# Hybrid attention step: the second weight block's split one token tile later and half of it on VectorE, the third tile's low parts ahead of the fourth tile's scaling, three filler products fewer

## The chip, the cores and the metric

The kernel runs on one core of a Trainium2 chip. The metric is the device time of one execution in microseconds (us). Three runs of the kernel before gave 967.75, 967.85 and 968.23 us; the median is 967.85 us.

## The reference, cut to what matters

One layer of a streaming encoder: RMS norm, one input projection, two kinds of attention, gates, an output projection and the residual. The change touches only the first part, in which 1024 prompt tokens and 64 sample tokens are normed and multiplied by the first two blocks of `w_in` columns:

```python
def rms_norm(x, w):
    xf = x.astype(jnp.float32)
    ms = jnp.mean(xf * xf, axis=-1, keepdims=True)
    return (xf * lax.rsqrt(ms + EPS)).astype(x.dtype) * w
...
    h = rms_norm(x, norm_w) @ w_in
    sb_q, sb_k, sb_v, sb_z, cb_q, cb_k, cb_v, cb_z, g_sb, g_cb = jnp.split(h, SPLIT_POINTS, axis=-1)
```

## The kernel before, in words

All products are made of fp32 values split in two: a high part (`xa`, `xm` for x; `whi`, `whix` for weights) and a low part, the rest (`xm`, `xb`; `wlo`, `wlox`). The names are shared: tile `xm` holds the low part of columns 0 to 511 and the high part of columns 512 to 1023. A product is high x high, low x high and high x low, so 24 instructions for one token tile and one block of 256 weight columns (8 slices of the contraction, three kinds), 16 for the sample tile.

The order of the work is the order of the code on each engine (the schedule is by hand); an engine takes its instructions in that order and waits at each for its inputs. The program begins with a phase in which the first weight block is multiplied while x is still being prepared:

- `beat(n)` (L447) puts n filler products of the identity on TensorE; a filler is two instructions. They wait for nothing and their result is not used.
- `prep_s(t)` (L261, L251, L252): ScalarE squares tile t and sums it, GpSimd turns the sum into the factor `rs`.
- `prep_a(t)` (L269): VectorE scales tile t by `rs` and the norm weights, in two halves of 512 columns, into `xn` (two buffers).
- `prep_b(t)` (L280, L288, L289): TensorE transposes `xn`, four 128x128 pieces for each half, into `pt` (two PSUM buffers, one per half); ScalarE copies a half out as the high part (L288), VectorE subtracts it from `pt` for the low part (L289). For the sample tile (t = 8) both parts go to `xs` (L283, L284).
- `W.hi` and `W.lo` (L117, L124) split a weight block: ScalarE makes the high part, GpSimd (or VectorE, if named) the low part. A block has two halves, `wraw` (rows 0 to 511 of `w_in`, giving `whi`, `wlo`) and `wrawx` (rows 512 to 1023, giving `whix`, `wlox`).

Block `i` runs over positions `ti` = 0 to 8, which are the token tiles 8, 0, 1, ... 7. While position `ti` of block 0 is multiplied, `ready(ti)` prepares token tile `ti` for the next position; a table gives the product number `m` before which it is put. "Tile 2" below is token tile 2, multiplied at position 3 and prepared during position 2. At the end of a position ScalarE takes the result out of PSUM (`vst`, L308). After positions 5 and 6 of block 0 the two halves of block 1 are split (L531), and the raw halves of block 2 are loaded through SyncE's queue. Block 1 begins with the sample tile.

Of the kernel before, what the change touches and what calls it, by code (L numbers as in the profile page):

```python
# [32 lines left out]
def hybrid_step_kernel(ctx: ExitStack, tc: tile.TileContext, x_prompt, x_sample, c_sbk, c_sbv, c_cbk, c_cbv,  # L33
# [3 lines left out]
    V, A, G, TE, SP = nc.vector, nc.scalar, nc.gpsimd, nc.tensor, nc.sync  # L37
# [15 lines left out]
    def rows(t):  # L53
        return 128 if t < 8 else NS
# [37 lines left out]
    def pad(pool, n):  # L92
        pool.tile([128, n // 4], F32, name=f"pad{n}", bufs=1)
# [37 lines left out]
    W = Weights()  # L131
# [69 lines left out]
    with ExitStack() as ph:  # L201
# [13 lines left out]
        def load_x(t):  # L215
            xt = p1.tile([128, D], F32, name="xt", bufs=4)
            SP.dma_start(xt[:rows(t)], tok(x_prompt, x_sample, t))
            xts[t] = xt
# [37 lines left out]
        def prep_s(t):  # L256
            r = rows(t)
            sq = p1.tile([128, D], F32, name="sq", bufs=1)
            ms = p1.tile([128, 1], F32, name="ms", bufs=4)
            rst[t] = p1.tile([128, 1], F32, name="rs", bufs=4)  # L260
            A.activation(sq[:r], xts[t][:r], AF.Square, accum_out=ms[:r])  # L261
            rsqrt(rst[t][:r], ms[:r], 1.0 / D, 1)

        def prep_a(t):
            r = rows(t)
            xt = xts.pop(t)
            xn = p1.tile([128, D], F32, name="xn", bufs=2)
            for c in (slice(0, 512), slice(512, D)):
                V.scalar_tensor_tensor(xn[:r, c], xt[:r, c], rst[t][:r], nw[:r, c], op0=OP.mult, op1=OP.mult)  # L269
            xns[t] = xn  # L270
# [3 lines left out]
        def prep_b(t):  # L274
            r = rows(t)
            xn = xns.pop(t)
            for hf in range(2):
                pt = psT.tile([128, 4, 128], F32, name="pt")
                for k in range(4):
                    TE.transpose(pt[:, k, :r], xn[:r, (hf * 4 + k) * 128:(hf * 4 + k + 1) * 128], ident[:r, :r])  # L280
                if t == 8:
                    s = xs[:, hf * 4:hf * 4 + 4]
                    A.activation(s[:, :, 0:64], pt[:, :, :r], AF.Copy)  # L283
                    V.tensor_tensor(out=s[:, :, 64:128], in0=pt[:, :, :r], in1=s[:, :, 0:64].bitcast(F32),  # L284
                                    op=OP.subtract)
                    continue
                h, l = (xhl[s][hf][:, :, xc(t):xc(t) + r] for s in range(2))
                A.activation(h, pt[:, :, :r], AF.Copy)  # L288
                V.tensor_tensor(out=l, in0=pt[:, :, :r], in1=h.bitcast(F32), op=OP.subtract)  # L289
# [155 lines left out]
        def beat(n):  # L445
            for k in range(n):
                TE.matmul(idle[:, k % 4], ident, ident, start=True, stop=True)  # L447
# [8 lines left out]
        for c in range(2):  # L456
# [1 line left out]
                TE.transpose(spread[c][:, k * 128:(k + 1) * 128],  # L458
                             nwt[:, 4 * c + k:4 * c + k + 1].to_broadcast([128, 128]), ident)
            V.tensor_copy(nw[:, c * 512:(c + 1) * 512], spread[c])  # L460
        beat(8)
        prep_s(8)
        prep_a(8)
        prep_s(0)
# [8 lines left out]
        pend, raw1 = [], None  # L473

        def ready(j):
            if 1 < j < 7:
                prep_a(j + 1)
            prep_b(j)
            if j == 0:
                prep_s(1)  # L480
            if j < 2:
                prep_a(j + 1)
            if j + 2 < 8:
                prep_s(j + 2)
            if j + 5 < 8:
                load_x(j + 5)

        def product(ps, t, ns, k, n, first, last):
            w = W.sp[i, k // 4][n // (ns - 1)][:, k % 4]
            x = xs[:, k] if t == 8 else xk(n % 2, k)[:, xc(t):xc(t) + rows(t)]  # L490
            TE.matmul(ps, x, w, start=first, stop=last)  # L491
        for i in range(nb):
            for ti, t in enumerate(TO):
                r = rows(t)
                last = (i, ti) >= (nb - 1, NT - 3)
                ps = (psA if ti % 3 == 2 and not last else psF).tile([128, 512], F32, name="acc")[:, :256]
                ns = 2 if t == 8 else 3
                steps = [(k, n) for k in range(KT) for n in range(ns)]
                if i == 0:
                    steps.sort(key=lambda e: (e[1], e[0]))  # L500
                    if ti == 0:
                        part8, steps = steps[12:], steps[:12]
                for m, (k, n) in enumerate(steps):
                    if i == 0 and m == (4, 20, 20, 16, 12, 8, 4, 0, -1)[ti]:
                        ready(ti)
                    if i == 0 and ti == 1 and m == 8:
                        for m8, e in enumerate(part8):
                            product(ps8, 8, 2, *e, False, m8 == 3)
                    product(ps, t, ns, k, n, m == 0, ti + i > 0 and m == len(steps) - 1)
                if i == 0 and ti == 0:  # L510
                    ps8 = ps
                    continue
                if i == 0 and ti == 1:
                    evac_nat(0, 8, ps8)
                if len(pend) >= 3 or (pend and pend[0][0] < i and ti > 3):
                    post_nat(*pend.pop(0))
                got = evac_nat(i, t, ps)
                if raw1:
                    norm_nat(*raw1)
                    pend.append(raw1[:3])  # L520
                raw1 = (i, t) + got if got else None
                if i == 0:
                    if ti == 2:
                        load_nat(1, 0)
                        load_nat(1, 1)
                        SP.dma_start(wqk[:, 0], q_norm_w[0:1, :].to_broadcast([128, 64]))
                        SP.dma_start(wqk[:, 1], k_norm_w[0:1, :].to_broadcast([128, 64]))
                if ti in (3, 6) and i > 0 or ti in (5, 6) and i == 0:
                    h = 1 if ti == 6 else 0
                    if i + 1 < nb:  # L530
                        W.split((i + 1, h))  # L531
                    if i + 2 < nb:
                        load_nat(i + 2, h)
                    elif h == 0:
                        load_raw(i + 2 - nb)
                if (i, ti) == (4, 2):
                    load_rb()
                if 0 <= 9 * i + ti - 40 < 8:
                    make_rb(9 * i + ti - 40)
                if i >= 5 and p1x is not None and not pend and not raw1 and ti >= 3:  # L540
                    p1x.close()
                    p1x = None
                    tp = sx.enter_context(tc.tile_pool(name="tp", bufs=1))
                    pad(tp, 64)
                    tms = [[tp.tile([128, 4, HF], F32R, name=f"t{n}{s}") for s in "hl"] for n in range(4)]
                    ws = sx.enter_context(tc.tile_pool(name="ws", bufs=3))
                    tq = ph.enter_context(tc.tile_pool(name="tq", bufs=3))
                    tjobs = iter(make_t(tms, tq))
                    tw = [3]
                if p1x is None:  # L550
                    tw[0] -= 1
                    if tw[0] < 0:
                        next(tjobs, None)
                if (i, ti) == (nb - 1, 5):
                    prep(0)
                if (i, ti) == (nb - 1, 6):
                    presum(1)
                if (i, ti) == (nb - 1, 7):
                    prep(1)
                if (i, ti) in ((0, 4), (2, 3)):  # L560
                    cache_load("sb" if i == 0 else "cb")
                at = {(1, 1): 0, (1, 4): 1, (1, 7): 2, (2, 1): 3}
                if (i, ti) in at:
                    cache_pair("sb", at[i, ti])
                if (i - 2, ti) in at:
                    cache_pair("cb", at[i - 2, ti])
                if (i, ti) in ((1, 1), (1, 5)):
                    for s in range(2):
                        h = ti // 4
                        for c in range(2):  # L570
                            o = 512 + c * HF
                            G.tensor_copy(xhl[s][h][:, :, o:o + 32],
                                          xs[:, 4 * h:4 * h + 4, 64 * s + 32 * c:64 * s + 32 * c + 32])
                if (i, ti) == (1, 0):
                    V.tensor_scalar(wqk[:, 0], wqk[:, 0], -0.125, None, op0=OP.mult)
# [6 lines left out]
    with ExitStack() as ph:  # L582
# [104 lines left out]
        for i in range(len(pairs)):  # L687
            bank, s1, u2, u3 = {}, {}, {}, {}
            for s in range(7):
# [11 lines left out]
                for c, (a, b) in enumerate(XC):  # L701
                    m = b - a
# [22 lines left out]
                if s == 4:  # L725
                    for c, (a, b) in enumerate(XC):
                        m = b - a
# [570 lines left out]
    for i in range(len(seq) + LAG + 2):  # L1298
        m = 0
# [13 lines left out]
        if i < len(seq):  # L1313
# [7 lines left out]
            m = int(acc) - emitted  # L1321
            emitted += m
        else:
            m = 8
# [306 lines left out]
```

## Time and profile before

| what | value |
|---|---|
| median of three runs | 967.85 us |
| the profiled execution | 967.6 us, of which the span of instructions is 965.8 us |
| TensorE busy | 957.4 us, 99% of the span |
| VectorE, ScalarE, GpSimd busy | 592.0, 475.9 and 395.1 us |
| granted TensorE clock | 1.0 throughout |
| block 0 and what prepares it | the first 44 us |

How to read the rows. A row of the timeline has the start and the length in us, the engine (PE TensorE, PEld its weight loads, DVE VectorE, ACT ScalarE, POOL GpSimd, SPq SyncE's queue), the line of the kernel, the operation, the tile written and those read, and how many like instructions are merged; in brackets how long the engine sat idle just before, and who ended that. Instructions of one engine overlap by about 0.1 us at their ends, so a row's length is a little more than the distance to the next row.

### The profile page before, as it was taken

To read this page: it belongs to the slowest core of one execution; us is meant where nothing else is said; L and a number is where in the kernel's file an instruction comes from. 1 tells how busy PE (TensorE), PEld (TensorE's weight loads), DVE (VectorE), ACT (ScalarE), POOL (GpSimd) and SP (SyncE) were. 2 spreads that over 40 slices of the span, in tenths; PEclk is the share of its full clock that TensorE was granted. 3 is DMA by queue.
4 is the path that set the end of the run, shared out by engine and by line. 5 is a ranking of instruction groups with operands and counts; after the bars stand their busy time and mean duration, and the time that the engine had idled before them with its cause. 6 is when DMAs were issued, how large, how long until landed. Compare 5 with 4: busy or idle time off the path is not lost.

```text
span 965.8 us, 20494 instructions
## 1 busy us (share of the span) xinstructions
PE 957.4 (99%) x7645; PEld 912.3 (94%) x7645; DVE 592.0 (61%) x1170; ACT 475.9 (49%) x1054; POOL 395.1 (41%) x392
## 2 busy tenths in 40 slices
PE   9999999999999999999999999999999999999998
PEld 8999999999999999999999988778888888999998
DVE  6556665696454555534332298777777765499735
ACT  6544443344444433333342277667887775465220
POOL 2276664115444566665542200002331111686651
PEclk9999999999999999999999999999999999999999
DMA  6727566534646564555522997769799932862642
GB/s 222 233 81 243 196 222 249 180 95 132 188 136 185 173 196 152 173 182 151 179 87 86 283 259 209 190 165 250 230 302 251 248 111 77 262 197 70 208 151 75
DMA packets 173384, 175.76 MB, mean 182 GB/s; under 512 B 30745, under 2 KB 157597, under 8 KB 173158
## 3 DMA queue, kind: packets, MB, share of 16 engines
q1 hardware_dynamic: 161734, 159.45, 55.9%
q10 hardware_dynamic: 8736, 8.33, 2.7%
q0 software_dynamic: 2816, 6.69, 2.1%
q8 instruction: 60, 0.98, 0.5%
q14 instruction: 38, 0.31, 0.1%
HBM read 112.42 MB, written 62.00 MB: 181 GB/s over the span
## 4 chain that ended last, share of the span: by engine, by line
PE 97%; ACT 1%; DVE 1%; issue 0%; DMA 0%; POOL 0%; POOLq 0%; ACTq 0%
PE b L708 30%; PE acc L491 19%; PE b L1545 8%; PE o L1225 7%; PE z L1133 7%; PE pt L1186 7%; PE acc L984 5%; PE b L1026 5%; PE acc L877 5%; PE pk L352 1%; PE acc L1581 1%; PE pc L447 1%; PE pt L280 0%; DVE xn L269 0%; PE acc L633 0%; PE pc L374 0%
## 5 line engine op out<-in xcount | busy, mean ns | idle before, releaser
L1186 PE MATMUL pt<-ident,be 128*128 128x128 f32 (+1 forms) x568 | 87.8, 279 | 0.6 <-ACT wT L1195 0.2
L1155 DVE TENSOR_TENSOR_SCAN be<-be,imp 128x128 f32<-128x128 f32 (+7 forms) x64 | 83.4, 1343 | 8.1 <-ACT be L1136 7.9
L1133 PE MATMUL z<-ks,sq 128*128 128x320 f32 (+5 forms) x384 | 87.5, 338 | 0.0
L1186 PEld LDWEIGHTS pt<-ident,be 128*128 128x128 f32 (+1 forms) x568 | 65.7, 140 | 13.0 <-issue 4.6
L1195 ACT ACTIVATE wT<-pt 128x512 f32<-128x512 f32 (+3 forms) x123 | 56.9, 496 | 42.8 <-PE pt L1186 42.7
L491 PE MATMUL acc<-whi,xa 128*128 128x256 f32 x256 | 70.7, 291 | 0.3 <-ACT xa L288 0.3
L716 DVE TENSOR_TENSOR u<-b,s 128x256 f32<-128x256 f32 (+1 forms) x56 | 24.3, 440 | 75.4 <-PE b L708 72.0
L491 PE MATMUL acc<-wlox,xm 128*128 128x256 f32 x256 | 67.7, 280 | 0.0
L491 PE MATMUL acc<-whix,xm 128*128 128x256 f32 x256 | 67.6, 279 | 0.0
L491 PE MATMUL acc<-whi,xm 128*128 128x256 f32 x256 | 67.6, 279 | 0.0
L491 PE MATMUL acc<-wlo,xa 128*128 128x256 f32 x256 | 67.6, 279 | 0.0
L491 PE MATMUL acc<-whix,xb 128*128 128x256 f32 x256 | 67.5, 279 | 0.0
L1133 PEld LDWEIGHTS z<-ks,sq 128*128 128x128 f32 x384 | 63.7, 190 | 1.7
L1225 PE MATMUL o<-wT,vp 128*64 128x256 f32 (+1 forms) x608 | 64.2, 357 | 0.0
L1225 PEld LDWEIGHTS o<-wT,vp 128*64 128x64 f32 x608 | 40.3, 137 | 23.6 <-issue 7.4
L1158 ACT ACTIVATE be<-be,sm 128x640 f32<-128x640 f32 (+5 forms) x68 | 47.2, 694 | 17.0 <-DVE sm L1157 16.9
L124 POOL TENSOR_TENSOR wlo<-wraw,whi 128x1024 fp32r<-128x1024 f32 x15 | 35.9, 2397 | 44.3 <-ACT whi L117 40.8
L781 POOL DMA_DIRECT2D d_osb<-zt x20 | 10.8, 540 | 101.5 <-DVE zt L1234 69.2
L437 POOL TENSOR_TENSOR whix<-ws,whix 128x512 fp32r<-128x512 f32 x28 | 36.9, 1317 | 34.5 <-ACT whix L436 34.5
L1146 ACT ACTIVATE be<-be,sm 128x640 f32<-128x640 f32 (+5 forms) x68 | 47.3, 696 | 5.2 <-DVE sm L1138 4.8
L1136 ACT ACTIVATE be<-z 128x384 f32<-128x384 f32 (+6 forms) x104 | 47.9, 514 | 3.2 <-PE z L1133 2.4
L491 PEld LDWEIGHTS acc<-whi,xa 128*128 128x128 f32 x256 | 46.4, 188 | 0.7 <-ACT xa L288 0.5
(315 smaller groups left out, 3194.7 us busy)
## 6 DMA issues: line engine op xcount, KB each, us to landing
wraw<-in_w_in_dram SPq DMA_DIRECT2D x31, 512.0 KB, 4.2
wrawx<-in_w_in_dram SPq DMA_DIRECT2D x17, 512.0 KB, 4.6
sq<-d_qsbT SPq DMA_DIRECT2D x32, 192.0 KB, 5.1
sq<-d_qcbT SPq DMA_DIRECT2D x32, 192.0 KB, 5.2
xt<-in_x_prompt_dram SPq DMA_DIRECT2D x8, 512.0 KB, 4.9
d_kcbT<-hl SPq DMA_DIRECT2D x8, 512.0 KB, 4.3
d_qcbT<-hl SPq DMA_DIRECT2D x8, 512.0 KB, 3.1
d_ksbT<-hl SPq DMA_DIRECT2D x16, 256.0 KB, 3.3
```

The costliest lines, as they stand in the source:

```text
L491: TE.matmul(ps, x, w, start=first, stop=last)
L708: TE.matmul(ps[:, :m], w[:, hl_, k], right[s](x)[:, k, a:b], start=s < 3 and k == 0 and e == 0, stop=k == 3 and e == 2, skip_group_check=s ...
L877: TE.matmul(ps[:, :b - a], w[:, k], xk(x, k)[:, a:b], start=k == 0 and n == 0, stop=k == KT - 1 and n == 2)
L984: TE.matmul(ps[:, :e - a], w[:, p, cw], g[:, a:e], start=m % 12 == 0, stop=m % 12 == 11)
L1026: TE.matmul(pp[uu][:, :n], w[:, p, uu * 128:uu * 128 + 128], g[:, a:e], start=p == 0 and m == 0, stop=p == NPAIR - 1 and m == 2)
L1133: TE.matmul(z[:, :m], s[:, e, q0:q0 + 128], ks[:, h, o + x:o + y], start=(e, h) == parts[0], stop=(e, h) == parts[-1])
L1136: A.activation(be[:r, x:y], z[:r, :m], AF.Sigmoid, scale=-0.125)
L1155: V.tensor_tensor_scan(be[:r, n - 1::-1], be[:r, n - 1::-1], im[:, ::-1], 0.0, op0=OP.mult, op1=OP.max)
L1186: TE.transpose(pt[:kr, x, :r], be[:r, kb * 128:kb * 128 + kr], ident[:r, :r])
L1195: A.activation(w[:, sl:sl + m, q0:q0 + r], pt[:, :m, :r], AF.Copy)
L1225: TE.matmul(o[hd * 64:hd * 64 + 64, c0:c1], vv[:kr, kb, hd * 64:hd * 64 + 64], wT[b, p, j, hd, s // 4][:kr, s % 4, c0:c1] if j < 4 else wT ...
L1545: TE.matmul(ps[:, t], left[s](xs_, k)[:, ts_], wt_[:, k], start=s < 3 and t == k == e == 0, stop=k == 3 and e == 2, skip_group_check=s > 2 ...
```

## The change

```diff
-        beat(8)
+        beat(5)
         prep_s(8)
         prep_a(8)
         prep_s(0)
...
         def ready(j):
-            if 1 < j < 7:
+            if 2 < j < 7:
                 prep_a(j + 1)
             prep_b(j)
             if j == 0:
                 prep_s(1)
-            if j < 2:
+            if j < 3:
                 prep_a(j + 1)
...
-                    if i == 0 and m == (4, 20, 20, 16, 12, 8, 4, 0, -1)[ti]:
+                    if i == 0 and m == (4, 20, 18, 14, 10, 6, 2, 0, -1)[ti]:
                         ready(ti)
...
-                if ti in (3, 6) and i > 0 or ti in (5, 6) and i == 0:
-                    h = 1 if ti == 6 else 0
+                if ti in (3, 6) and i > 0 or ti in (6, 7) and i == 0:
+                    h = 1 if ti == (6 if i else 7) else 0
                     if i + 1 < nb:
-                        W.split((i + 1, h))
+                        W.split((i + 1, h), V if i == 0 and h else None)
```

Four things change, all in block 0. Three of eight filler products ahead of the sample tile's transposes go. `prep_a(3)` comes behind `prep_b(2)` instead of ahead of it. `ready` comes two products earlier in positions 2 to 6. The two halves of block 1 are split after positions 6 and 7 instead of 5 and 6, the second half's low part by VectorE; the loads of block 2's raw halves, which stand behind each split, move with them.

On VectorE around tiles 2 and 3, the difference of the two programs (`xn` is the scaled tile, `fl` the sample tile's result, L289 the low parts of one tile):

```order
 L296 TENSOR_TENSOR fl<-acc,fl 64x256
-L269 SCALAR_TENSOR_TENSOR xn<-xt,rs,nw 128x512 x2
 L289 TENSOR_TENSOR xm<-pt,xa 128x4x128
 L289 TENSOR_TENSOR xb<-pt,xm 128x4x128
-L269 SCALAR_TENSOR_TENSOR xn<-xt,rs,nw 128x512 x2
+L269 SCALAR_TENSOR_TENSOR xn<-xt,rs,nw 128x512 x4
 L289 TENSOR_TENSOR xm<-pt,xa 128x4x128
 L289 TENSOR_TENSOR xb<-pt,xm 128x4x128
```

The scaling of tile 3, which stood ahead of the low parts of tile 2, now stands behind them and right ahead of the scaling of tile 4.

On TensorE in positions 2 and 3 (L280 are the transposes, of tile 2 and then of tile 3; each L491 row of four is one kind of product for half of the contraction):

```order
-L491 MATMUL acc<-wlo,xa 128x256 x4
+L491 MATMUL acc<-wlo,xa 128x256 x2
 L280 MATMUL pt<-ident,xn 128x128 x8
+L491 MATMUL acc<-wlo,xa 128x256 x2
 L491 MATMUL acc<-wlox,xm 128x256 x4
 L491 MATMUL acc<-whi,xa 128x256 x4
 L491 MATMUL acc<-whix,xm 128x256 x4
 L491 MATMUL acc<-whi,xm 128x256 x4
-L491 MATMUL acc<-whix,xb 128x256 x4
+L491 MATMUL acc<-whix,xb 128x256 x2
 L280 MATMUL pt<-ident,xn 128x128 x8
+L491 MATMUL acc<-whix,xb 128x256 x2
```

Each set of eight transposes stands two products further forward; no product is added or lost.

On ScalarE at the end of block 0 (`vst` takes out a position's result, L288 makes a tile's high parts, L117 the weights' high parts):

```order
 L308 ACTIVATE vst<-acc 128x256
-L117 ACTIVATE whi<-wraw 128x1024
 L288 ACTIVATE xa<-pt 128x4x128
 L288 ACTIVATE xm<-pt 128x4x128
 L308 ACTIVATE vst<-acc 128x256
-L117 ACTIVATE whix<-wrawx 128x1024
+L117 ACTIVATE whi<-wraw 128x1024
 L288 ACTIVATE xa<-pt 128x4x128
 L288 ACTIVATE xm<-pt 128x4x128
-L308 ACTIVATE vst<-acc 128x256 x2
+L308 ACTIVATE vst<-acc 128x256
+L117 ACTIVATE whix<-wrawx 128x1024
```

The first half's high part moves from ahead of tile 6's high parts to ahead of tile 7's, the second half's from there to behind both. The low parts that follow them stand last in this phase on their engines: `wlo` is GpSimd's only one now, and `wlox` is VectorE's, behind the low parts of tile 7.

## The prediction

> **What bounds the kernel now.** I read the page's first part, then its chain of work, then the timeline of the first 46 us, where the whole change lies.
>
> ```profile
> span 965.8 us, 20494 instructions
> PE 957.4 (99%) x7645; PEld 912.3 (94%) x7645; DVE 592.0 (61%) x1170; ACT 475.9 (49%) x1054; POOL 395.1 (41%) x392
> ...
> PE 97%; ACT 1%; DVE 1%; issue 0%; DMA 0%; POOL 0%; POOLq 0%; ACTq 0%
> ```
>
> TensorE is busy for 957.4 of 965.8 us and holds 97% of the chain. A change outside its products can win only what TensorE waits. Whatever reaches TensorE in block 0 goes on to the end, because nothing behind it waits for a clock of its own: what is gained or lost by 44 us is the answer. So I look for TensorE's waits there, in three places.
>
> The start:
>
> ```profile
> 2.01 0.43 SPq L111 DMA_DIRECT2D wraw<-in_w_in_dram  x1
> ...
> 5.87 2.47 PE L447 MATMUL pc<-ident 128*128 128x128 f32 x16
> ...
> 6.72 1.40 DVE L269 SCALAR_TENSOR_TENSOR xn<-xt,rs,nw 64x512 f32<-64x512 f32 x2
> ...
> 8.27 0.71 PE L280 MATMUL pt<-ident,xn 64*128 64x64 f32 x8
> 8.78 0.66 ACT L283 ACTIVATE xs<-pt 128x256 fp32r<-128x256 f32 x2 [1.19 <-PE pt L280]
> ...
> 9.32 1.06 ACT L117 ACTIVATE whi<-wraw 128x1024 fp32r<-128x1024 f32 x1
> 9.86 1.41 DVE L269 SCALAR_TENSOR_TENSOR xn<-xt,rs,nw 128x512 f32<-128x512 f32 x2
> ...
> 10.43 0.74 PE L491 MATMUL acc<-whi,xs 128*128 128x256 f32 x4 [0.58 <-ACT whi L117]
> ...
> 12.32 1.22 DVE L124 TENSOR_TENSOR wlox<-wrawx,whix 128x1024 fp32r<-128x1024 f32 x1
> ```
>
> The sample tile's scaling ends at 8.12 (6.72 + 1.40), its first half at about 7.45. The transposes that need it start at 8.27, with no idle time ahead of them: they stood behind the fillers, which fill TensorE from 5.87. Then all is one chain: transposes, ScalarE's copies at 8.78, the weights' high part at 9.32, the first product at 10.43.
>
> Tiles 2 and 3:
>
> ```profile
> 19.21 0.94 POOL L252 TENSOR_TENSOR rs<-rs,half 128x1 f32<-128x1 f32 x1
> ...
> 19.63 1.03 PE L280 MATMUL pt<-ident,xn 128*128 128x128 f32 x8
> 19.66 0.41 DVE L296 TENSOR_TENSOR fl<-acc,fl 64x256 f32<-64x256 f32 x1
> ...
> 20.10 0.42 ACT L308 ACTIVATE vst<-fl 64x256 f32<-64x256 f32 x1 [1.08 <-DVE fl L296]
> 20.18 1.41 DVE L269 SCALAR_TENSOR_TENSOR xn<-xt,rs,nw 128x512 f32<-128x512 f32 x2
> ...
> 20.54 0.39 ACT L308 ACTIVATE vst<-acc 128x256 f32<-128x256 f32 x1
> ...
> 20.82 0.59 ACT L288 ACTIVATE xa<-pt 128x512 fp32r<-128x512 f32 x1
> ...
> 21.46 0.74 PE L491 MATMUL acc<-whi,xa 128*128 128x256 f32 x4 [0.33 <-ACT xa L288]
> 21.51 0.69 DVE L289 TENSOR_TENSOR xm<-pt,xa 128x512 fp32r<-128x512 f32 x1
> ...
> 22.11 0.68 DVE L289 TENSOR_TENSOR xb<-pt,xm 128x512 fp32r<-128x512 f32 x1
> ...
> 23.29 0.55 POOL L252 TENSOR_TENSOR rs<-rs,half 128x1 f32<-128x1 f32 x1
> ...
> 23.48 1.03 PE L280 MATMUL pt<-ident,xn 128*128 128x128 f32 x8
> ...
> 24.27 0.72 PE L491 MATMUL acc<-wlo,xa 128*128 128x256 f32 x4
> ```
>
> TensorE waits 0.33 us at 21.46 for tile 2's high part, which ScalarE begins at 20.82, right behind two result copies; the first of these waited 1.08 us for VectorE's `fl`.
>
> Tile 7:
>
> ```profile
> 33.65 3.56 DVE L269 SCALAR_TENSOR_TENSOR xn<-xt,rs,nw 128x512 f32<-128x512 f32 x2 [0.63 <-POOL rs L252]
> ...
> 34.27 2.40 POOL L124 TENSOR_TENSOR wlo<-wraw,whi 128x1024 fp32r<-128x1024 f32 x1 [0.66 <-ACT whi L117]
> ...
> 35.41 0.64 PE L491 MATMUL acc<-wlo,xa 128*128 128x256 f32 x4
> ...
> 35.88 0.63 PE L491 MATMUL acc<-wlox,xm 128*128 128x256 f32 x4
> ...
> 36.83 1.05 ACT L117 ACTIVATE whix<-wrawx 128x1024 fp32r<-128x1024 f32 x1
> ...
> 37.13 0.68 DVE L289 TENSOR_TENSOR xm<-pt,xa 128x512 fp32r<-128x512 f32 x1
> ...
> 37.87 1.25 PE L280 MATMUL pt<-ident,xn 128*128 128x128 f32 x8 [1.36 <-DVE xm L289]
> 37.95 2.38 POOL L124 TENSOR_TENSOR wlox<-wrawx,whix 128x1024 fp32r<-128x1024 f32 x1 [1.29 <-ACT whix L117]
> ...
> 38.88 0.71 PE L491 MATMUL acc<-whi,xa 128*128 128x256 f32 x4
> 39.19 0.69 DVE L289 TENSOR_TENSOR xm<-pt,xa 128x512 fp32r<-128x512 f32 x1 [0.78 <-ACT xa L288]
> ```
>
> The largest wait, 1.36 us. Tile 7's scaling takes 3.56 us where every other tile's takes 1.41, because GpSimd's split runs from 34.27 to 36.67 in the middle of it. Tile 6's low parts are queued behind it, and tile 7's transposes need the PSUM buffers that these free.
>
> **The change part by part**, in us, minus a gain, against the profiled execution's 967.6 (span 965.8 and 1.8 around it). That is 0.25 below the median of the runs shown, 967.85, to which I refer the result.
>
> (a) *Three fillers fewer: -0.4.* They are six instructions.
>
> ```profile
> 5.87 1.06 PE L447 MATMUL pc<-ident 128*128 128x128 f32 x4
> ```
> ```profile
> 6.72 1.62 PE L447 MATMUL pc<-ident 128*128 128x128 f32 x12
> ```
>
> The first four start 0.21 apart (0.85 / 4), the other twelve 0.13 on average (8.27 - 6.72 = 1.55). Ten end at about 6.72 + 6 x 0.13 = 7.5, so 0.77 of filler goes. The transposes' first half then starts at 7.5, the second when VectorE is done, about 8.2, and needs half of 0.71: 8.6 instead of 8.98. That is 0.4, the rest of the 0.77 becomes waiting for the scaling. ScalarE's second copy, `whi` and the first product follow: 10.43 becomes 10.05. VectorE's scaling of tile 0 (9.86) comes 0.4 sooner as well, so tile 1's chain follows. `wraw` must have landed by 8.94:
>
> ```profile
> DMA to landing us min/median/max: 5.8/6.2/6.6
> ```
>
> Issued at 2.01, it lands by 8.6 even at the longest of these. Bounds: 0 if something else held the chain, -0.77 if all the filler counted.
>
> [...]
>
> (b) *Transposes two products earlier: 0.* In position 2 they would start 0.24 sooner, but ScalarE's high part of tile 2 starts at 20.82 behind the result copies, not behind the transposes. That chain (tile 2's scaling, `fl`, two copies) isn't touched, so the 0.33 stays. Bounds: 0 to -0.33. Later positions have slack either way.
>
> (c) *Tile 3's scaling behind tile 2's low parts: +0.5.* Tile 2's first low part can begin only when `xa` ends at 21.41, so it moves from 21.51 to 21.44: a gain of 0.07 that no product needs. The scaling moves from 20.18 to behind the second low part, 22.65, and ends its halves at 23.4 and 24.06 (1.41). Tile 3's transposes, now two products earlier, are due at 23.48 - 0.24 = 23.24: four start at 23.5, four at 24.17, and products go on at about 24.53, where without a wait it were 24.03. So 0.5 lost. Tile 4's scaling then follows, and tile 3's low parts, late by up to 0.6, are still ahead of the products that read them. Next late is nothing. `xt` of tile 7 is loaded when tile 3's scaling has freed its buffer, about 1 us later; SyncE's result stores and the raw loads of block 1 are queued behind it, and the split is a position later. Bounds: +0.2 (the first half's wait alone) to +1.0 (GpSimd's `rs` of tile 4 collides with the scaling and holds it: at 19.21 it took 0.94 beside one, not 0.55).
>
> (d) *The split a position later: -1.7.* Without GpSimd in its way tile 7's scaling takes 1.41: 33.65 to 35.06, tile 6's low parts end at about 35.7 and 36.3. TensorE reaches the transposes at 36.35 (35.88 + 4 x 0.118, the distance from 35.41 to 35.88 being four products), half by half, and finds both buffers free. Eight transposes take 0.79 without a wait (23.48 to 24.27), so the products of position 7 go on at 37.15, not 38.88: 1.73. I keep 1.7. Bounds: -1.36 (the named wait alone) to -1.73.
>
> What the split now lies beside: ScalarE does `whi` at about 36.9 ahead of tile 7's high parts, which so end at 39; they are first read at 40, after 24 products of position 7. GpSimd's `wlo` then runs beside tile 7's low parts; the row at 39.19 shows that these, which read PSUM, take 0.69 beside such a split as well. `whix` waits for position 7's result, 40.7 to 41.7, and VectorE's `wlox` takes 1.22 (as at 12.32 for block 0), to 42.95.
>
> ```profile
> 45.50 0.29 PE L491 MATMUL acc<-wlox,xs 128*128 128x256 f32 x1
> ```
>
> It is first read here, which becomes about 43.9: cover of 0.9. The load of block 2's second raw half is issued some 2.5 us later, since `wlox` must have read the old one; it is used only at the end of block 1.
>
> Sum: -0.4 + 0 + 0.5 - 1.7 = -1.6. From 967.6 this gives 966.0; from the median of runs, **966.2**, 0.17% less.
>
> **The rivals.**
>
> *Start worth more (965.5).* The step from 0.21 to the full rate comes later in a typical run than in the profiled one. If it came behind all sixteen filler instructions, these would end at 9.3 (5.87 + 16 x 0.213) instead of 8.27, 1.0 later, while ten end at 8.0 at the latest, before the scaling at 8.12. A typical run would then lose between 0 and 1.0 more than the profiled one, and the change returns it; I take 0.7. For it: the runs spread by 0.5 (967.75 to 968.23), and the profiled one is below all. Against: nothing shows that the spread lies there. Also in this case: (c) at its low bound.
>
> *Gain given back (967.1).* (c) at +1.0 and (a) near -0.1: -0.8. For it: VectorE's queue from 22 to 26 has two scalings in a row with GpSimd's `rs` between. Against: two products more lie between these transposes and the next tile.
>
> *The fillers were needed (969.8, slower).* TensorE's products stay at half rate. The place is 7.5 to 15.9; there stand 36 products of block 0, each then 0.1 dearer (0.21 for 0.118): +3.6 on 966.2. It decides if the step has not come when the fillers end at 7.5 and waits and transposes do not count for it. Against: the step comes soon after 6.72, ahead of 7.5, and a wait of 1.36 at 37.87 changes no rate behind it. [...]
>
> *It doesn't do what it says.* (b) and the first half of (c) are this already: what the named low parts gain is 0.07.
>
> **How the numbers follow.** Forecast 966.2 with its own range of 965.9 to 966.9: 0.55. Start worth more: 0.27. Given back: 0.14. Slower: 0.04. The range leaves out the slower case and half of the tails: 965.3 to 967.3. A measurement of this kernel tells about 0.2% (1.9 us) from no change, so faster begins at 965.9. To faster go the second case and a tenth of the first's edge, 0.30; to slower 0.04; the rest, 0.66, is within.
>
> **What would show it.** (a) The transposes at 8.27 split in two, the second set at about 8.2, and the first product at 10.05. (b) The 0.33 at the head of position 3 stays. (c) A new wait of TensorE for `xn` at tile 3's transposes, two pieces, 0.5 in all. (d) No VectorE scaling over 1.5 us, no TensorE wait at position 7, `wlox` on VectorE of 1.22 without a waiter. Wrong would make it: TensorE waiting at block 1's first products for `wlox`, a wait behind 46 us that wasn't there, or products 0.21 apart after 7.5.

## The result and the profile after

The changed kernel takes 966.40 us (median of 17 runs), the kernel before 968.26 us in the same series (17 runs). The ratio is 0.9982, 95% interval 0.9975 to 0.9989: 1.7 us less, within the 0.2% (1.9 us) that the prediction set as the bound of "no change". A second series of the same two kernels gave 966.28 and 967.71 us, ratio 0.9985 (0.9976 to 0.9994). The forecast was 1.65 us less, so its sum stands. Its shares do not all stand, as the experiments show.

The first part of the page and its chain of work, kernel after:

```profile
span 966.1 us, 20485 instructions
...
PE 958.3 (99%) x7639; PEld 913.0 (94%) x7639; DVE 591.4 (61%) x1171; ACT 476.2 (49%) x1054; POOL 391.9 (41%) x391
...
PE 97%; ACT 1%; DVE 0%; DMA 0%; issue 0%; POOL 0%; ACTq 0%
```

TensorE bounds it as before. The span is 0.3 us *longer* than before's 965.8, and this execution took 967.92 us, not 966.4. The reason lies far behind the change. These are one group of products of the stage of line 708, with first and last start in us, of before, of after, and of a second profile of the same changed kernel (`after_2`):

```profile
L708 PE MATMUL b<-xa,whi x224: 275/290/369, 226.6 to 506.0; 128*128 128x256 f32 x56, 128*128 128x288 f32 x56
```
```profile
L708 PE MATMUL b<-xa,whi x224: 276/290/367, 225.3 to 506.1; 128*128 128x256 f32 x56, 128*128 128x288 f32 x56
```
```profile
L708 PE MATMUL b<-xa,whi x224: 276/290/367, 225.2 to 504.5; 128*128 128x256 f32 x56, 128*128 128x288 f32 x56
```

The stretch is 279.4, 280.8 and 279.3 us long. The changed kernel arrives 1.3 us early, and this one execution loses 1.5 us in a stage that the change does not touch; the second profile keeps the lead. So block 0 is read apart from the rest, and a single execution's total is no measure of this change.

The start, after. The first row is ScalarE's square of the sample tile, which begins when that tile has landed:

```profile
4.81 1.06 ACT L261 ACTIVATE sq<-xt 64x1024 f32<-64x1024 f32 x1 [2.15 <-DMA xt<-in_x_sample_dram]
5.87 1.39 PE L447 MATMUL pc<-ident 128*128 128x128 f32 x10
...
7.73 0.47 PE L280 MATMUL pt<-ident,xn 64*128 64x64 f32 x4 [0.47 <-DVE xn L269]
8.39 0.46 PE L280 MATMUL pt<-ident,xn 64*128 64x64 f32 x4 [0.20 <-DVE xn L269]
...
10.27 0.74 PE L491 MATMUL acc<-whi,xs 128*128 128x256 f32 x4 [0.56 <-ACT whi L117]
```

The transposes wait for VectorE in two sets, as foretold. The first product comes at 10.27 against 10.43, not at 10.05. The tile landed 0.39 later than in before, and the transposes now wait for what hangs on it; in `ab` below, where this square begins at 4.36, the first product does come at 10.05. Before had

```profile
4.42 1.06 ACT L261 ACTIVATE sq<-xt 64x1024 f32<-64x1024 f32 x1 [1.77 <-DMA xt<-in_x_sample_dram]
```

Tiles 2 and 3, after:

```profile
21.25 0.74 PE L491 MATMUL acc<-whi,xa 128*128 128x256 f32 x4 [0.25 <-ACT xa L288]
...
22.44 1.41 DVE L269 SCALAR_TENSOR_TENSOR xn<-xt,rs,nw 128x512 f32<-128x512 f32 x2
...
23.32 0.94 POOL L252 TENSOR_TENSOR rs<-rs,half 128x1 f32<-128x1 f32 x1
23.33 1.29 PE L280 MATMUL pt<-ident,xn 128*128 128x128 f32 x8
...
24.38 0.48 PE L491 MATMUL acc<-whix,xb 128*128 128x256 f32 x2
...
25.64 0.63 PE L491 MATMUL acc<-whi,xa 128*128 128x256 f32 x4
```

and the row of before that answers to the last one:

```profile
25.29 0.63 PE L491 MATMUL acc<-whi,xa 128*128 128x256 f32 x4
```

Position 3 took 25.29 - 21.46 = 3.83 us and takes 25.64 - 21.25 = 4.39: 0.56 lost, spent at tile 3's transposes, which start late and take 1.29 instead of 1.03. The scaling starts 1.19 behind the head of the position, exactly where the prediction put it (22.65 - 21.46). GpSimd's `rs` does collide with it, but it is `rs` that takes 0.94; the scaling keeps its 1.41.

Tile 7, after:

```profile
33.75 1.41 DVE L269 SCALAR_TENSOR_TENSOR xn<-xt,rs,nw 128x512 f32<-128x512 f32 x2 [0.61 <-POOL rs L252]
...
36.27 0.64 PE L491 MATMUL acc<-wlox,xm 128*128 128x256 f32 x4
36.75 1.03 PE L280 MATMUL pt<-ident,xn 128*128 128x128 f32 x8
...
37.54 0.72 PE L491 MATMUL acc<-whi,xa 128*128 128x256 f32 x4
...
41.98 1.23 DVE L124 TENSOR_TENSOR wlox<-wrawx,whix 128x1024 fp32r<-128x1024 f32 x1 [1.89 <-ACT whix L117]
...
44.17 0.29 PE L491 MATMUL acc<-wlox,xs 128*128 128x256 f32 x1
```

From the last four products ahead of the transposes to the first behind them it was 38.88 - 35.88 = 3.00 us; now it is 37.54 - 36.27 = 1.27: 1.73 gone, as foretold. `wlox` ends at 43.21 and is read at 44.17 without a wait.

### The profile page after: what moved, and what is told of

Same layout as the page of the kernel before. It is cut to its first block, busy times and chain, and to the rows that moved or that the text cites. A ratio compares the mean times of both kernels' runs of the same rounds, so it can differ in the third digit from the quotient of the medians.

```text
span 966.1 us, 20485 instructions
## 1 busy us (share of the span) xinstructions
PE 958.3 (99%) x7639; PEld 913.0 (94%) x7639; DVE 591.4 (61%) x1171; ACT 476.2 (49%) x1054; POOL 391.9 (41%) x391
## 4 chain that ended last, share of the span: by engine, by line
PE 97%; ACT 1%; DVE 0%; DMA 0%; issue 0%; POOL 0%; ACTq 0%
PE b L708 30%; PE acc L491 20%; PE b L1545 8%; PE o L1225 7%; PE z L1133 7%; PE pt L1186 7%; PE acc L984 5%; PE b L1026 5%; PE acc L877 5%; PE pk L352 1%; PE pt L280 1%; PE acc L1581 1%; PE acc L633 0%; DMA xt<-in_x_sample_dram 0%; PE pc L374 0%; DVE xn L269 0%
## 5 line engine op out<-in xcount | busy, mean ns | idle before, releaser
L491 PE MATMUL acc<-whi,xa 128*128 128x256 f32 x256 | 70.9, 291 | 0.2 <-ACT xa L288 0.2
L491 PE MATMUL acc<-whix,xm 128*128 128x256 f32 x256 | 67.7, 279 | 0.0
L491 PE MATMUL acc<-whi,xm 128*128 128x256 f32 x256 | 67.7, 279 | 0.0
L491 PE MATMUL acc<-wlo,xa 128*128 128x256 f32 x256 | 67.7, 279 | 0.0
L491 PE MATMUL acc<-whix,xb 128*128 128x256 f32 x256 | 67.6, 279 | 0.0
L491 PE MATMUL acc<-wlox,xm 128*128 128x256 f32 x256 | 67.6, 279 | 0.0
L491 PEld LDWEIGHTS acc<-whi,xa 128*128 128x128 f32 x256 | 46.5, 188 | 0.6 <-ACT xa L288 0.4
```

## The experiments

The theory was the prediction's: four separate terms, (a) -0.4, (b) 0, (c) +0.5, (d) -1.7. The rivals were that the start is worth more, that the gain is given back around tile 3, and, once the first runs were seen, that tile 7's stall was never (d)'s to remove. The traces are compared by four numbers that no later stage touches: when the sample tile's square starts, when block 0's first product starts, when block 1's does, and the distance between these two.

| kernel | square | first product | block 1 | distance |
|---|---|---|---|---|
| before | 4.42 | 10.43 | 44.42 | 33.99 |
| ctl_before | 4.61 | 10.26 | 44.26 | 34.00 |
| a_fillers | 5.01 | 10.47 | 44.41 | 33.94 |
| c_order | 4.78 | 10.89 | 45.36 | 34.47 |
| d_split | 4.50 | 10.62 | 43.08 | 32.46 |
| b_table | 4.77 | 10.75 | 42.92 | 32.17 |
| bc_order | 4.49 | 10.03 | 42.84 | 32.81 |
| after | 4.81 | 10.27 | 43.10 | 32.83 |
| after_2 | 4.72 | 10.18 | 43.01 | 32.83 |
| no_c | 4.74 | 10.20 | 42.47 | 32.27 |
| no_c_early | 4.57 | 10.06 | 42.78 | 32.72 |
| d_gpsimd | 4.62 | 10.09 | 42.77 | 32.68 |
| a_none | 4.71 | 10.39 | 45.22 | 34.83 |
| ab | 4.36 | 10.05 | 42.16 | 32.11 |

Each ratio below is to the kernel before, run beside it on the same chip.

**ctl_before**: the kernel before, unchanged, as a measure of what a repeat gives.

> The kernel before, unchanged, once more. My theory: ratio 1.000 within 0.05%; the stage of the input projection from about 226 us on (line 708) comes in two lengths, 297.3 or 298.8 us, whatever the program, so here too it may be either. Rival: the longer stage, seen only in the profile after, is set by the change; then this kernel shows 297.3 in every execution and its times form one group.

Measured: 967.48 against 967.57, ratio 0.9998 (0.9989 to 1.0006). The distance repeats to 0.01 us, and the stage of line 708 has its short length, 297.3. The first product does not repeat:

```profile
5.87 2.30 PE L447 MATMUL pc<-ident 128*128 128x128 f32 x16
8.11 0.71 PE L280 MATMUL pt<-ident,xn 64*128 64x64 f32 x8
```

The same sixteen filler instructions take 2.30 here and 2.47 in the first profile, and all behind them moves by 0.17.

**a_fillers**: (a) alone.

```diff
-        beat(8)
+        beat(5)
```

> Only the three fillers less (eight become five), all else as before. My theory: -0.2 to -0.9 us (0.02 to 0.09%), the first product of block 0 at 10.05 to 10.3 instead of 10.43, the sample tile's transposes waiting for VectorE's scaling. Rival 1 (nothing behind the fillers was waiting for them): 0. Rival 2 (the fillers were needed for the rate): products 0.21 us apart behind 7.5 us, over 1 us slower.

Measured: 967.39 against 967.57, ratio 0.9999 (0.9991 to 1.0008).

```profile
5.01 1.06 ACT L261 ACTIVATE sq<-xt 64x1024 f32<-64x1024 f32 x1 [2.34 <-DMA xt<-in_x_sample_dram]
...
7.93 0.47 PE L280 MATMUL pt<-ident,xn 64*128 64x64 f32 x4 [0.47 <-DVE xn L269]
8.59 0.46 PE L280 MATMUL pt<-ident,xn 64*128 64x64 f32 x4 [0.20 <-DVE xn L269]
...
10.47 0.74 PE L491 MATMUL acc<-whi,xs 128*128 128x256 f32 x4 [0.55 <-ACT whi L117]
```

The wait has moved from the fillers to VectorE, and the tile landed 0.6 later than in before, so this profile shows no gain at all. The table sorts it out. From square to first product, the seven profiles with five fillers have 5.46 four times, 5.47, 5.49 and 5.69 (mean 5.50); the six with eight have 5.54 to 6.12 (mean 5.90). By this measure (a) is worth 0.40 on average, between about 0.1 and 0.65 in one execution. The measure suits the kernels with five fillers, which mostly wait for the tile; with eight it is the fillers that the first product waits for. Their length varies from 1.96 (bc_order) to 2.94 us (c_order), and the first product comes 2.15 to 2.26 behind the start of the transposes that follow them in all six. The first product's own start is 10.19 on average with five and 10.50 with eight, which gives 0.31. So (a) is worth 0.3 to 0.4, too little for these times to tell.

**bc_order**: (b) and (c), with the fillers and the split as before.

```diff
-            if 1 < j < 7:
+            if 2 < j < 7:
...
-            if j < 2:
+            if j < 3:
...
-                    if i == 0 and m == (4, 20, 20, 16, 12, 8, 4, 0, -1)[ti]:
+                    if i == 0 and m == (4, 20, 18, 14, 10, 6, 2, 0, -1)[ti]:
```

> Only the order: tile 3's scaling behind tile 2's low parts, and the table with ready two products earlier. My theory: +0.55 us (0.06% slower), TensorE waits for xn at tile 3's transposes, in two pieces, and the wait of 0.33 for tile 2's high part stays at 0.2 to 0.33. Rival (the low parts' earlier place helps): that wait goes and the kernel is 0.3 us faster.

Measured: 966.55 against 967.57, ratio 0.9988 (0.9979 to 0.9997). By my terms these two parts alone should cost 0.5; they gain 1. Tile 7's stall is gone though the split stands where it stood:

```profile
33.50 1.42 DVE L269 SCALAR_TENSOR_TENSOR xn<-xt,rs,nw 128x512 f32<-128x512 f32 x2 [0.61 <-POOL rs L252]
...
34.40 2.77 POOL L124 TENSOR_TENSOR wlo<-wraw,whi 128x1024 fp32r<-128x1024 f32 x1 [0.93 <-ACT whi L117]
```

Scaling and split still meet, but now GpSimd pays: its split takes 2.77 instead of 2.40, with cover to spare, and the scaling takes 1.42. With this the theory of separate terms fell.

**d_split**: (d) alone.

```diff
-                if ti in (3, 6) and i > 0 or ti in (5, 6) and i == 0:
-                    h = 1 if ti == 6 else 0
+                if ti in (3, 6) and i > 0 or ti in (6, 7) and i == 0:
+                    h = 1 if ti == (6 if i else 7) else 0
...
-                        W.split((i + 1, h))
+                        W.split((i + 1, h), V if i == 0 and h else None)
```

> Only the split of block 1 a position later with its second low part on VectorE. My theory: -1.7 us (0.18% faster), tile 7's scaling takes 1.41 instead of 3.56, no TensorE wait at position 7, none at block 1's first products. Rival (part of it comes back as a wait for wlox or for tile 7's high parts, now behind whi on ScalarE): -0.8 us, with a TensorE wait between 38 and 46 us.

Measured: 966.27 against 967.57, ratio 0.9986 (0.9977 to 0.9995).

```profile
33.85 1.41 DVE L269 SCALAR_TENSOR_TENSOR xn<-xt,rs,nw 128x512 f32<-128x512 f32 x2 [0.62 <-POOL rs L252]
...
36.07 0.64 PE L491 MATMUL acc<-wlox,xm 128*128 128x256 f32 x4
36.55 1.03 PE L280 MATMUL pt<-ident,xn 128*128 128x128 f32 x8
37.34 0.72 PE L491 MATMUL acc<-whi,xa 128*128 128x256 f32 x4
```

37.34 - 36.07 = 1.27, so (d) alone removes the 1.73 too. The distance shrank by only 1.53: behind 37.34 four products took 0.47 instead of 0.455 in this execution. Either part is enough; the question became which of the two is free.

**b_table**: (b) alone, the table's line of the diff above.

> Only the table: ready two products earlier in positions 2 to 6; fillers, order and split as before. My prediction had 0 for this. New theory: in the kernel before, GpSimd's split began 0.05 us ahead of the second half of tile 7's scaling and held it up; with ready two products earlier, the scaling is ahead of the split and the 1.36 us wait is gone without moving the split: -1.7 us, tile 7's scaling at 1.41, GpSimd's first low part of block 1 longer than 2.4. Rival (in the run with order and table it was the order's delay that turned this): -0.1 us, and the wait at tile 7 stays.

Measured: 966.42 against 967.71, ratio 0.9984 (0.9975 to 0.9993).

```profile
33.73 1.42 DVE L269 SCALAR_TENSOR_TENSOR xn<-xt,rs,nw 128x512 f32<-128x512 f32 x2 [0.61 <-POOL rs L252]
...
34.57 2.84 POOL L124 TENSOR_TENSOR wlo<-wraw,whi 128x1024 fp32r<-128x1024 f32 x1 [0.87 <-ACT whi L117]
```
```profile
36.12 0.62 PE L491 MATMUL acc<-wlox,xm 128*128 128x256 f32 x4
36.58 1.03 PE L280 MATMUL pt<-ident,xn 128*128 128x128 f32 x8
37.37 0.71 PE L491 MATMUL acc<-whi,xa 128*128 128x256 f32 x4
```

37.37 - 36.12 = 1.25, and the distance is 1.82 shorter than before's. One line of numbers brings all that (d) was to bring.

**c_order**: (c) alone, the two conditions on `prep_a` above.

> Only the order: tile 3's scaling behind tile 2's low parts; fillers, table and split as before. Theory: +0.4 to +0.55 us for the wait at tile 3's transposes (here two products later, so a shorter wait than with the table), and the wait of 1.36 us at tile 7 stays, because both engines there are delayed alike. Rival (the delay turns the order of scaling and split): the wait at tile 7 goes, about -1.2 us.

Measured: 968.58 against 967.71, ratio 1.0009 (1.0001 to 1.0018). The distance grows by 0.48, and the stall stays:

```profile
34.54 3.61 DVE L269 SCALAR_TENSOR_TENSOR xn<-xt,rs,nw 128x512 f32<-128x512 f32 x2 [0.60 <-POOL rs L252]
...
35.21 2.40 POOL L124 TENSOR_TENSOR wlo<-wraw,whi 128x1024 fp32r<-128x1024 f32 x1 [0.70 <-ACT whi L117]
```

So of bc_order's two parts it was the table. The traces also show how narrow it is. A scaling is two instructions, and the second starts 0.67 behind the first in all of them. In before it started at 34.31, 0.05 behind GpSimd's split (34.27), and took 2.90 instead of 0.75; ctl_before and a_fillers have the same 0.05. Here both start at 35.21, and again it is the scaling that is held. In b_table it started at 34.40, and the split came 0.16 behind it, at 34.57. The table brings tile 7's factor `rs` and its scaling two products forward (0.24; the measured shift is 0.21) against the split, which hangs on position 5's result. The traces show both outcomes. In before and here the split keeps its 2.40, and the scaling takes 3.56 and 3.61 and ends 0.54 behind it; in b_table and bc_order, where the scaling was first, it keeps its 1.42, and the split takes 2.84 and 2.77. So the one that started first kept its length, and at the one tie it was the split; why one holds the other is not shown.

**no_c**: the changed kernel with (c) undone.

```diff
-            if 2 < j < 7:
+            if 1 < j < 7:
...
-            if j < 3:
+            if j < 2:
```

> The changed kernel with tile 3's scaling put back ahead of tile 2's low parts; fillers, table and split as changed. My theory: 0.55 us below the changed kernel, so -2.2 to -2.4 us against before (0.23 to 0.25%), no wait at tile 3's transposes, the wait of 0.25 to 0.33 for tile 2's high part still there. Rival (the low parts' place matters): no better than the changed kernel, -1.7 to -1.9, with a wait for a low part in position 3.

Measured: 966.68 against 969.16, ratio 0.9972 (0.9961 to 0.9982).

```profile
21.18 0.75 PE L491 MATMUL acc<-whi,xa 128*128 128x256 f32 x4 [0.25 <-ACT xa L288]
...
22.96 1.03 PE L280 MATMUL pt<-ident,xn 128*128 128x128 f32 x8
...
25.01 0.63 PE L491 MATMUL acc<-whi,xa 128*128 128x256 f32 x4
```

Position 3 is back to 25.01 - 21.18 = 3.83, the transposes take 1.03 without a wait, and the distance is 0.56 shorter than after's. That is (c)'s price. The times can't tell: the kernel before has a median of 969.16 in this series, 1.6 above the 967.57 of the first experiments, so a ratio of this series (no_c, no_c_early, d_gpsimd, a_none) is not to be set beside those of the others.

**no_c_early**: no_c, with the sample tile's result taken out earlier, to remove the 0.25 us at 21.18 that stands behind those copies.

```diff
+                    if i == 0 and ti == 1 and m == 16:
+                        evac_nat(0, 8, ps8)
...
-                if i == 0 and ti == 1:
-                    evac_nat(0, 8, ps8)
```

> As the kernel above, and the sample tile's result is taken out at product 16 of position 1, ahead of tile 1's transposes, instead of at that position's end. My theory: the wait for tile 2's high part comes from the result copies, so it goes (0.25 to 0.33 us): -2.5 to -2.7 us against before. Rival (the wait comes from the transposes' own distance, which the table's two products were to lengthen): it stays, and the time is that of the kernel above.

Measured: 966.68 against 969.16, ratio 0.9978 (0.9969 to 0.9987), no better than no_c, and the distance is 0.45 longer. The wait at the head of position 3 goes; two others come:

```profile
16.13 0.42 ACT L308 ACTIVATE vst<-fl 64x256 f32<-64x256 f32 x1 [1.15 <-DVE fl L296]
...
17.23 0.74 PE L491 MATMUL acc<-whi,xa 128*128 128x256 f32 x4 [0.21 <-ACT xa L288]
...
20.26 1.41 DVE L269 SCALAR_TENSOR_TENSOR xn<-xt,rs,nw 128x512 f32<-128x512 f32 x2 [0.44 <-POOL rs L252]
...
21.59 0.68 DVE L289 TENSOR_TENSOR xm<-pt,xa 128x512 fp32r<-128x512 f32 x1
...
22.33 0.53 PEld L491 LDWEIGHTS acc<-whi,xm 128*128 128x128 f32 x4 [0.29 <-DVE xm L289]
```

The copy now stands ahead of tile 1's high part, which TensorE waits for. And in position 3 a weight load waits 0.29 us for tile 2's low part, which VectorE makes behind tile 3's scaling; that position takes 4.18 us (21.14 to 25.32) instead of 3.83. This is the order that (c) turns round. So (c) answers a wait that these traces show only where the copy is early; the two together were not run, and whether they pay stays open.

**d_gpsimd**: the changed kernel with both low parts on GpSimd, the split a position later all the same.

```diff
-                        W.split((i + 1, h), V if i == 0 and h else None)
+                        W.split((i + 1, h))
```

> The changed kernel with both low parts of block 1 on GpSimd. My theory: wlox starts with whix's end at 41.95, takes 2.4 instead of 1.22 and ends at 44.4, while it is first read at 44.17: TensorE waits 0.2 to 0.3 there, so 0.25 us slower than the changed kernel. Rival (VectorE is what the part on the split is worth): 1 us slower or more, with waits beyond that one.

Measured: 968.19 against 969.16, ratio 0.9984 (0.9976 to 0.9993).

```profile
41.70 2.40 POOL L124 TENSOR_TENSOR wlox<-wrawx,whix 128x1024 fp32r<-128x1024 f32 x1 [1.25 <-ACT whix L117]
...
44.15 0.39 PE L491 MATMUL acc<-wlox,xs 128*128 128x256 f32 x1
```

GpSimd ends `wlox` at 44.10, and the product that reads it would have started at 43.85 (the one ahead started at 43.73): a wait of 0.3 us in block 1. VectorE's half spares this, and it is needed only because the split was moved: at its old place GpSimd ends `wlox` at 40.60 (b_table) and nobody waits.

**a_none**: the changed kernel with none of these five fillers, to see from where fewer fillers cost the clock.

```diff
-        beat(5)
```

> The changed kernel with none of the remaining five fillers there. My theory: TensorE is idle from 5.9 to 7.7 either way for the scaling, so if the rate steps up as before, the time is the same within 0.3 us. Rival (the fillers were needed for the rate): products stay 0.21 us apart behind 7.7 for 3 us or more, 1 to 3.6 us slower than the changed kernel.

Measured: 969.34 against 969.16, ratio 1.0004 (0.9994 to 1.0014), so the whole gain is gone; in the traces its distance is 0.84 longer than before's.

```profile
7.63 0.47 PE L280 MATMUL pt<-ident,xn 64*128 64x64 f32 x4 [2.10 <-DVE xn L269]
8.29 0.68 PE L280 MATMUL pt<-ident,xn 64*128 64x64 f32 x4 [0.20 <-DVE xn L269]
8.91 1.65 PE L447 MATMUL pc<-ident 128*128 128x128 f32 x6
10.39 1.23 PE L490 MATMUL acc<-whi,xs 128*128 128x256 f32 x4
...
14.83 0.74 PE L490 MATMUL acc<-whi,xa 128*128 128x256 f32 x4
```

The lines behind the edit are numbered one less. Four products take 1.23 instead of 0.74, and only from 14.83 on are they at 0.74 again. This profile's granted clock is 0.50 from 8.23 to 15.05 us, where the other profiles have 1.00; the distance is 2.0 longer than after's. "The fillers were needed" is real, with its point somewhere between five fillers and none. Five left at most 0.87 us idle ahead of the transposes (in no_c), and no profile with five shows a product of block 0 at half rate.

**ab**: (a) and (b), with neither (c) nor (d), which by the results above is all that should pay.

> Three fillers less and the table, without the order and with the split where it was. Theory: the split's later place and VectorE's half of it bring nothing once the table is there, so this is 0.55 us below the changed kernel of the same call and equal within 0.2 to the one with fillers, table and split. Rival (the split's place is worth its 1.7 us by itself): 1 us slower than the changed kernel.

Measured: 965.62 against 967.71, ratio 0.9979 (0.9970 to 0.9988).

```profile
32.98 1.41 DVE L269 SCALAR_TENSOR_TENSOR xn<-xt,rs,nw 128x512 f32<-128x512 f32 x2 [0.61 <-POOL rs L252]
```

The shortest distance of all, 32.11, and the lowest median. b_table differs from it by (a) alone: its median is 0.80 higher, and its first product comes at 10.75 instead of 10.05. no_c differs from it by (d) alone and has 32.27: given (b), (d) brings nothing. (Of the 0.16, part is pace: between 33.5 and 35.5 us the products stand 0.118 apart in no_c and 0.113 in ab.)

**after_2**: the changed kernel again, beside ab and before.

> The changed kernel once more, beside the three others on one chip. Theory: block 1 begins 32.8 us after the first product, as in its first profile (34.0 before), and 0.55 us later than in the kernels without the order; the input projection's stage is 297.3 or 298.8 us long, either one. Rival: that stage is 298.8 again, set by the change.

Measured: 966.28 against 967.71, ratio 0.9985 (0.9976 to 0.9994). Its distance equals after's, 32.83. ab's median is 0.66 lower, and eight of its ten runs lie below the lowest of these eleven (966.05). The traces agree with 0.72 of distance, of which 0.56 is (c). So ab is the better one.

## Why the prediction was right, and which step was not

The time was right: 0.17% less was foretold, 0.18% and 0.15% were measured in the two series. By the traces the sum is 0.3 to 0.4 for (a) and 1.16 of distance (33.99 to 32.83), 1.5 to 1.6 us against the 1.6 of the prediction. That it held although (b) was misread is luck in part: what (b) brings is the same wait that (d) had been credited with. Had the two removed different waits, the sum would have missed what (b) brings.

- **(a)** -0.4: about right as a mean (0.3 to 0.4), with the mechanism named: the rest of the filler's time becomes waiting for the scaling. The landing of the sample tile spreads by as much (square at 4.36 to 5.01), which I did not count; so 10.05 was missed in a profile that has the gain, and met in ab.
- **(b)** 0: this step failed. I looked for what the earlier transposes bring at position 3 and found that chain unmoved, rightly: the wait went from 0.33 only to 0.25. I wrote that later positions have slack either way, and did not follow the scaling of tile 7, which the same line moves by 0.21 against the split that was 0.05 ahead of it.
- **(c)** +0.5: 0.56 between after and no_c, 0.48 between before and c_order and 0.64 between b_table and bc_order, at the place and with the rows foretold. The scaling's start was right to 0.01, and `rs` pays the collision, so the upper bound of 1.0 was not reached.
- **(d)** -1.7: the stall is worth 1.73, but the credit was wrong. (d) alone removes it (d_split) and so does (b) alone (b_table); beside (b), (d) earns nothing (ab against no_c) and needs VectorE for `wlox`. I treated 3.56 as the price of running beside a split, where it was the price of losing one start to it.

Of the rivals, *start worth more* named a real spread: the step from 0.21 to 0.11 us falls early or late in the fillers from run to run (at 5.9 us in bc_order, 7.9 in c_order). But it supposed that a typical run loses 0.7 more there than the profiled one; the profiled one's sixteen filler instructions took 2.47, and the mean of the six profiles with eight fillers is 2.52. *Gain given back* did not come, since (c) stayed at 0.48 to 0.64. *The fillers were needed* holds for none (granted clock 0.50 from 8.23 to 15.05 us in a_none), not for five. That (b) and half of (c) *do not do what they say* is half true: (b)'s named waits hardly change, and it carries the gain by another way.

## What to carry to other kernels

Here a shift of 0.21 us between two starts took the scaling from 3.56 to 1.42 us, so where a trace shows an instruction stretched by a neighbour, read the two start times before costing any cure: the split led by only 0.05 us, and moving one a little against the other was enough. When a change has several parts that could each remove one wait, credit the wait once, and try each part alone; here one line of a table and three fillers kept the whole gain (965.62 us), and of the rest one part cost 0.56 us and one brought nothing. Where single executions differ by 1.5 us, compare stretches that only the change touches.

## What the hardware showed that I had not expected

- **The clock fell back behind a stretch of waits and transposes.** In a_none TensorE has 2.10 us without an instruction, then transposes, and the granted clock is 1.00 from 4.82 to 8.23, 0.50 to 15.05 and 1.00 behind that. In before, 1.36 us idle at 37.87 left it at 1.00. The wait in a_none ends at 7.63, 0.60 ahead of the fall. Whether its length, the transposes or something else set the clock back is not shown.
- **The step to full rate wanders.** TensorE's instructions ahead of the first product go from 0.21 to 0.11 apart at 4.8 us in a_none, at 5.9 in bc_order, at 7.0 in before and at 7.9 in c_order; the sixteen filler instructions take 2.94 there and 1.96 in bc_order. Each trace's record of the granted clock begins at this step, so the 1.0 of the table for the kernel before holds from 7.0 us on. The 14 profiles spread over 3.1 us; what sets the moment is not shown.
- **One stage has two lengths.** The stage of line 708 is 1.5 us longer in 3 of 14 profiles (after, no_c_early and d_gpsimd), with the same instructions and no new wait. The loss is not at one place: in after it grows evenly against after_2, by about 0.08 in each 12 us, from some 65 us behind the stage's start to its end. What sets the length stays open. The program alone does not, since after_2 is the same kernel as after. But all three are among the five profiles that have both five fillers and the later split, and whether these make the longer one more frequent is not shown. The kernel before moved by as much between two series (medians of 967.57 and 969.16), without a trace of the second.
